# A due-time planner that keeps transfers in order: its backward pass, two TensorE costs and one buffer's clock changed

## The chip, the cores and the metric

The kernel runs on 1 core of one Trainium2 chip. The time is the device time of one execution in microseconds (us). Engines: PE is TensorE, DVE VectorE, ACT ScalarE, POOL GpSimd; SP is SyncE, whose queue issues nearly all DMA transfers.

## The reference

One decoder step on 512 prompt tokens and 8 sample tokens (one new token of each of 8 sequences with 2048 past tokens), all in float32:

```python
h = rmsnorm(x); z = h @ w_in                      # 1024 -> 2840 columns
q, ck, cv, sk, sv, wk, wv, gate, dq, dk, dv = split(z)
o_nsa  = gate0 * compressed + gate1 * selected + gate2 * window   # 8 heads, blocks chosen by top-k
o_diff = rmsnorm((softmax(Q1 K1) - lam * softmax(Q2 K2)) V)       # 4 heads
x = x + concat(o_nsa, o_diff) @ w_out
u = rmsnorm(x) @ w_up; c = causal_conv3(u); a, b = split(c)
x = x + (silu(a) * b) @ w_down
y = rmsnorm(x)                                    # and the new K/V rows and conv states
```

The sample tokens attend to paged caches (16 pages of 128 tokens per sequence, found through a page table): K and V pages of the differential heads, pages of the compressed and selected branches, and a window buffer.

## The kernel before, in words

Activations lie transposed, 520 token columns in two halves of 260. Each float32 operand is split into a high and a low part (xh, xl; wh, wl), and each product is three matmuls: xh wh, xl wh, xh wl. A tile of weights (128 columns of w_in, 512 KB) is loaded into one of three raw buffers (wr, ring RAWR), ACT copies its high part (wh), and DVE or POOL subtracts that for the low part (wl) into a ring of pairs (WH). The in-projection has 22 such tiles and one of the gate (w_g).

Beside the in-projection, PE takes the scores of the sample queries on the K pages (Qzd on kp; 128 pages of 256 KB, two to a kp tile, 7 kp tiles in ring KS), and behind it those on the cp pages (Qzs on cp) and the compression of the cp pages: products of split pages (wh, wl) with w1h and w1l, 256 columns each, and narrow rows of the prompt's own compression (phk with w1h and w1l, 132 and 66 columns). Then come attention, V pages (vp), and the out-projection. From there on (`wout`, `up`, `down`, from L2305) the code is in a fixed order.

All that is ahead of it is written as generators ("processes", `p_...`), each of which yields steps: an engine, a model duration, and the events it sets. `p_wraw` (L909) loads weights, `p_wprep` (L922) splits them, `p_inproj` (L977) multiplies, `p_kload` (L1003) loads K pages, `p_k` (L1017) scores four of them a step, `p_load` (L1217) loads cp pages, `p_stage2` (L1182) small weights, `p_vload` V pages, `p_win` the window buffer. Class `Issue` (L257) runs them on a model of the engines: `run` (L355) takes, among the steps of the engine that is free first, the one with the least `urgency` (L347), that is, its due time from the plan, for PE with a price for a turn from one kind of matmul to another. `used` (L691) tells the model from when on a buffer that the hand-written start has used is free.

`latest` (L403) makes the due times: it goes backward through the steps done, and gives each the latest start with which the model's end stays the same:

```python
        late, free, plan = [end] * len(self.done), dict.fromkeys(self.free, end), {}
        for n in range(len(self.done) - 1, -1, -1):
            name, k, eng, t0, t1, after = self.done[n]
            t = late[n] - (t1 - t0)
            free[eng] = plan[name, k] = t
            for m, lag in after:
                late[m] = min(late[m], t - lag)
```

Only dependences count there: `free` is written and not read, so two transfers on one queue may get the same due time. `kernel` (at the end of the file) builds the program 8 times with the plan of the time before, then 60 times with the best plan and random changes of its due times (0.3 us), and issues the one with the least model end.

Of the kernel before, what the change touches and what calls it, by code (L numbers as in the profile page):

```python
# [41 lines left out]
T_G = 22  # L42
# [214 lines left out]
class Issue:  # L257
# [15 lines left out]
            "qp": 0.14}  # L273
    STICK = 30.0

    IDLE = 0.15

    def __init__(self, plan=None, stuck=False):
# [76 lines left out]
    def run(self):  # L355
        while self.procs:
            ready = []
            for p in list(self.procs):
                if p["op"] is None:
                    if not self.ready(p):  # L360
                        continue
                    self.step(p)
                    if p["op"] is None:
                        continue
                ops = p["op"][0]
                o = min(ops, key=lambda o: self.start(p, o) + o[1]) if isinstance(ops, list) else ops
                ready.append((self.start(p, o), p, o))
            if not ready:
                if self.stuck:
                    raise Planned(float("inf"), None)  # L370
                raise RuntimeError("the processes wait for one another" + str([
                    (p["name"], p["gen"].gi_frame.f_code.co_name, p["gen"].gi_frame.f_lineno,
                     p["gen"].gi_yieldfrom and p["gen"].gi_yieldfrom.gi_frame.f_code.co_name,
                     p["gen"].gi_yieldfrom and p["gen"].gi_yieldfrom.gi_frame.f_lineno)
                    for p in self.procs if p["op"] is None]))
            first = min(ready, key=lambda x: x[0])
            t, p, o = min((x for x in ready if x[2][0] == first[2][0] and x[0] <= first[0] + self.IDLE),
                          key=lambda x: (self.urgency(x[1], x[2], x[0]), x[0], x[1]["name"]))
            sets = p["op"][1:]
            o[2]()  # L380
            end = t + o[1]
            if o[0] == "pe":
                end += self.turn(p)
                self.last = self.KIND.get(p["gen"].__name__, "r")
            self.free[o[0]] = end
            if self.shares(o):
                self.port = end

            if p["of"] is not None:
                p["after"].append((p["of"], (self.AFTER[p["eng"]] if p["eng"] != o[0] else 0.0) + p["pause"]))  # L390
            n = len(self.done)
            self.done.append((p["name"], p["k"], o[0], t, end, p["after"]))
            p["after"], p["pause"], p["of"], p["k"] = [], 0.0, n, p["k"] + 1
            p["t"], p["eng"], p["op"] = end, o[0], None
            for s in sets:
                if isinstance(s, Slot):
                    s.got.t = -50.0
                else:
                    s.t, s.eng, s.of = end, o[0], n
            self.now = end  # L400
            self.step(p)

    def latest(self):  # L403

        end = max(d[4] for d in self.done)
        late, free, plan = [end] * len(self.done), dict.fromkeys(self.free, end), {}
        for n in range(len(self.done) - 1, -1, -1):
            name, k, eng, t0, t1, after = self.done[n]
            t = late[n] - (t1 - t0)
            free[eng] = plan[name, k] = t  # L410
            for m, lag in after:
                late[m] = min(late[m], t - lag)
        return plan
# [7 lines left out]
def _build(tc, T, plan, last):  # L421
# [3 lines left out]
    def mm(out, l, r, start, stop):  # L425
        te.matmul(out, l, r, start=start, stop=stop)  # L426
# [59 lines left out]
    def ps(role):  # L486
        b = ROLE[role][turn[role] % len(ROLE[role])]
        turn[role] += 1
        return PSP(f"bank{b}", [128, 512])
# [137 lines left out]
    t0, t1, t2 = ORDER[:3]  # L627
# [55 lines left out]
    WH, HX, QU, RAWR, ZR, TM, SQ = Ring(2), Ring(2), Ring(4), Ring(3), Ring(3), Ring(2), Ring(2)  # L683
# [4 lines left out]
    def E(*key):  # L688
        return ev.setdefault(key, Event())

    def used(ring, n, t=None):  # L691

        slots = [ring.slot() for _ in range(n)]
        for sl in slots:
            sl.got.t, sl.done.t = -50.0, t
        return slots
# [244 lines left out]
    def new_z(t):  # L941

        if t in T_Q:
            return qu[T_Q.index(t)], None
        if t in T_DV or t in (T_SV, T_WV):
            return zst[t], None
        return None, ZR.slot()

    def blocks(acc, t, hf, ks):
        wh, wl = prep[t]  # L950
        c = slice(hf * HC, (hf + 1) * HC)
        if t == T_G:

            for k in ks:
                w = slice(k * 64, k * 64 + 56)
                mm(acc[:56, :HC], wh[:, w], xh[:, k, c], k == 0, False)
                mm(acc[:56, :HC], wh[:, w], xl[:, k, c], False, k == KT - 1)
            return
        for k in ks:
            w = slice(k * 128, k * 128 + 128)  # L960
            mm(acc[:, :HC], wh[:, w], xh[:, k, c], k == 0, False)
            mm(acc[:, :HC], wh[:, w], xl[:, k, c], False, False)
            mm(acc[:, :HC], wl[:, w], xh[:, k, c], False, k == KT - 1)

    def p_evac(t, z, zsl, accs, slots):
        m = 56 if t == T_G else 128
        if zsl:
            yield zsl
            zsl.got.t = -50.0
            z = X("z", [128, NT], F32, 3)  # L970
        for hf in (1, 0):
            c = slice(hf * HC, (hf + 1) * HC)
            yield E("accs", t, hf)
            yield ("dve", tdve(HC), lambda: tt(ve, z[:m, c], accs[hf][:m, :HC], rstd[:m, c], OP.mult), PS), slots[hf].done
        yield from p_after(t, z, zsl)

    def p_inproj():  # L977
        for n in range(3, NIN):
            t = ORDER[n]
            z, zsl = new_z(t)  # L980
            accs, slots = {}, {}
            if n > 3:
                yield E("w", n)
            for hf in (1, 0):
                sl = slots[hf] = ACC.slot()
                yield sl
                for k in range(KT):
                    def f():
                        if k == 0:
                            accs[hf] = ps("acc")  # L990
                        blocks(accs[hf], t, hf, [k])
                    sets = (sl,) if k == 0 else ()
                    if k == KT - 1:
                        sets = (E("accs", t, hf),) + ((whslot[n].done,) if hf == 0 else ())
                    yield (("pe", 0.24 if t == T_G else 0.36, f),) + sets
                if hf:
                    Q.spawn(p_evac(t, z, zsl, accs, slots), 1, Q.now, "pe")


    kslots, kslot = {}, {}  # L1000
# [14 lines left out]
    NKP = 2  # L1015

    def p_k():  # L1017
        for h in range(4):
            yield E("Qzd", h)
        for i in range(0, NSLOT, NKP):  # L1020
            qd, b = i // 16, (i // 2) % 8
            if i % 16 == 0:
                sl = KB.slot()
                yield sl
                box = {}
            for n in range(i, i + NKP):
                yield E("kp", n)

            def f():
                if i % 16 == 0:  # L1030
                    box["p"] = ps("k")
                for n in range(i, i + NKP):
                    hf = n % 2
                    for h in range(4):
                        mm(box["p"][32 * h:32 * h + 32, 256 * hf:256 * hf + 256], Qzd[:, h, 32 * b:32 * b + 32],
                           kslots[n][:, :, h * 128:(h + 1) * 128], b == 0 and hf == 0, b == 7 and hf == 1)
            yield ((("pe", 0.45 * NKP + 0.1, f),) + tuple(kslot[n].done for n in range(i, i + NKP))
                   + ((sl,) if i % 16 == 0 else ()))
            if (i + NKP) % 16 == 0:
                Q.spawn(p_kout(qd, box["p"], sl), 2, Q.now, "pe")  # L1040

        def f():
            KR.close()
            RAW[0] = Pool(tc, "R0", side="right")
        yield (None, 0.0, f), E("R0")

    def p_kout(qd, kd, sl):
        yield ("act", tact(512), lambda: act(Sd[:, 512 * qd:512 * qd + 512], kd)),
        yield ("dve", tdve(512), lambda: ve.tensor_reduce(out=fac[:, qd:qd + 1], in_=kd, axis=AX.X, op=OP.max), PS), \
            sl.done, E("kd", qd)  # L1050
# [72 lines left out]
    blocks(acc0[t2, 1], t2, 1, range(KT))  # L1123
    used(RAWR, 3, -10.0)
    used(RAWR, 1, -2.2)
    used(WH, 3, -5.0)
    whslot[3] = used(WH, 1)[0]
    used(KS, 4, -10.0)
    used(ZR, 4, -10.0)
# [1446 lines left out]
```

## Time and profile before

| | |
|---|---|
| median of 3 runs | 923.12 us (922.76 to 923.97) |
| profiled execution | 923.06 us |
| its span | 921.2 us |
| its mean granted clock of PE | 0.990 |
| PE busy | 899.1 us |
| DVE, ACT, POOL busy | 573.5, 384.4, 168.3 us |
| bytes moved | 179.83 MB, mean 195 GB/s |

The span runs from the first to the last instruction; the execution has 1.9 us around it. A row of a timeline has its start, its length, engine, line, operation, output and inputs, the number of instructions it stands for, and in brackets how long the engine stood idle before it and what ended that. Matmuls overlap: a row's length is longer than the distance to the next one.

### The profile page before, as it was taken

How to read it: one execution, taken by the hardware profiler on the slowest of the kernel's cores; microseconds unless marked ns; L12 is line 12 of the kernel's file. 1: busy time of each engine (PE TensorE's matmuls, PEld its weight loads, DVE VectorE, ACT ScalarE, POOL GpSimd, SP SyncE). 2: the span in 40 equal slices, each digit the busy share in tenths (PEclk: the TensorE clock that was granted, in tenths of full speed). 3: DMA queues.
4: the chain of work that ended last, by engine and by line, in shares of the span. 5: the costliest groups of instructions: out<-in, count | busy, mean ns of one | idle time of the engine just before them, and what ended most of it. 6: DMA issues, size and time to landing. Idle time of an engine off the chain costs nothing.

```text
span 921.2 us, 22310 instructions
## 1 busy us (share of the span) xinstructions
PE 899.1 (98%) x8628; PEld 805.7 (87%) x8628; DVE 573.5 (62%) x1362; ACT 384.4 (42%) x790; POOL 168.3 (18%) x342
## 2 busy tenths in 40 slices
PE   8999999999999999999998999999999999999996
PEld 5998888889999856656578999999999999999995
DVE  7697563365768696768854667777777777311233
ACT  5256331254555564565652234444444444211120
POOL 5221110000111100101113442111112121224230
PEclk9999999989999999999999999999999999999998
DMA  7749999997777599898733522222222222433322
GB/s 265 241 145 369 347 361 354 320 297 240 227 244 229 207 372 376 291 338 286 246 123 134 150 95 102 92 93 92 93 92 93 92 93 63 151 105 119 104 76 94
DMA packets 86060, 179.83 MB, mean 195 GB/s; under 512 B 10049, under 2 KB 28994, under 8 KB 85954
## 3 DMA queue, kind: packets, MB, share of 16 engines
q1 hardware_dynamic: 85954, 178.41, 56.4%
q8 instruction: 68, 1.11, 0.5%
q14 instruction: 38, 0.31, 0.1%
HBM read 165.78 MB, written 12.59 MB: 194 GB/s over the span
## 4 chain that ended last, share of the span: by engine, by line
PE 89%; DMA 4%; DVE 3%; issue 2%; SPq 1%; ACT 1%; POOL 0%; POOLq 0%; DVEq 0%
PE bank L426 85%; PE bank L1896 3%; DMA kp<-in_kpg 2%; SPq L527 1%; DMA kcT<-vn 1%; DVE bank L1835 1%; DMA cp<-in_cpg 1%; DMA wr<-in_w_in 0%; PE bank L557 0%; DMA vp<-in_vpg 0%; DVE y L438 0%; PE bank L1707 0%; DVE wl L435 0%; ACT gh L429 0%; ACT xh L429 0%
## 5 line engine op out<-in xcount | busy, mean ns | idle before, releaser
L426 PE MATMUL bank<-gl,wh 128*128 128x260 f32 x704 | 199.0, 283 | 0.0
L426 PE MATMUL bank<-gh,wl 128*128 128x260 f32 x704 | 198.9, 283 | 0.0
L426 PE MATMUL bank<-gh,wh 128*128 128x260 f32 x704 | 198.9, 282 | 0.0
L429 ACT ACTIVATE wh<-wr 128x1024 fp32r<-128x1024 f32 (+2 forms) x94 | 96.9, 1030 | 190.2 <-PE bank L426 162.8
L435 DVE TENSOR_TENSOR wl<-wr,wh 128x1024 fp32r<-128x1024 f32 (+1 forms) x86 | 111.2, 1293 | 95.9 <-ACT wh L429 95.5
L426 PEld LDWEIGHTS bank<-gh,wh 128*128 128x128 f32 x704 | 132.6, 188 | 0.0
L426 PEld LDWEIGHTS bank<-gl,wh 128*128 128x128 f32 x704 | 132.5, 188 | 0.0
L426 PEld LDWEIGHTS bank<-gh,wl 128*128 128x128 f32 x704 | 132.4, 188 | 0.0
L426 PE MATMUL bank<-xh,wh 128*128 128x260 f32 (+1 forms) x368 | 105.5, 289 | 1.1 <-ACT wh L429 1.1
L426 PE MATMUL bank<-xl,wh 128*128 128x260 f32 (+1 forms) x368 | 104.5, 286 | 1.8 <-DVE xl L438 1.7
L426 PE MATMUL bank<-xh,wl 128*128 128x260 f32 x352 | 100.1, 284 | 0.0
L426 PE MATMUL bank<-hh,wh 128*128 128x260 f32 (+2 forms) x340 | 96.3, 283 | 0.0
L426 PE MATMUL bank<-hh,wl 128*128 128x260 f32 (+2 forms) x340 | 96.1, 283 | 0.0
L426 PE MATMUL bank<-hl,wh 128*128 128x260 f32 (+2 forms) x340 | 96.0, 282 | 0.0
L426 PEld LDWEIGHTS bank<-xh,wh 128*128 128x128 f32 (+1 forms) x368 | 68.9, 187 | 6.8 <-issue 4.5
L438 DVE SCALAR_TENSOR_TENSOR c<-u,cvw,c 128x536 f32<-128x536 f32 x88 | 69.6, 791 | 2.8 <-ACT c L429 1.3
L426 PEld LDWEIGHTS bank<-xl,wh 128*128 128x128 f32 (+1 forms) x368 | 68.9, 187 | 2.6 <-DVE xl L438 2.5
L426 PEld LDWEIGHTS bank<-xh,wl 128*128 128x128 f32 x352 | 66.9, 190 | 0.0
L426 PEld LDWEIGHTS bank<-hh,wl 128*128 128x128 f32 x340 | 64.1, 188 | 0.0
L426 PEld LDWEIGHTS bank<-hh,wh 128*128 128x128 f32 x340 | 64.0, 188 | 0.0
L441 DVE TENSOR_TENSOR u<-bank,rst 128x260 f32<-128x260 f32 x132 | 40.0, 333 | 38.6 <-PE bank L426 33.0
L426 PEld LDWEIGHTS bank<-hl,wh 128*128 128x128 f32 x340 | 64.0, 188 | 0.0
(392 smaller groups left out, 1913.3 us busy)
## 6 DMA issues: line engine op xcount, KB each, us to landing
vp<-in_vpg SPq DMA_DIRECT2D x128, 320.0 KB, 5.5
kp<-in_kpg SPq DMA_DIRECT2D x128, 256.0 KB, 5.4
cp<-in_cpg SPq DMA_DIRECT2D x128, 192.0 KB, 3.9
wr<-in_w_up SPq DMA_DIRECT2D x44, 512.0 KB, 3.2
wr<-in_w_in SPq DMA_DIRECT2D x21, 512.0 KB, 5.5
wr<-in_w_down SPq DMA_DIRECT2D x16, 512.0 KB, 3.4
out_zT<-z SPq DMA_DIRECT2D x14, 260.0 KB, 5.5
wr<-in_w_down SPq DMA_DIRECT2D x8, 384.0 KB, 3.1
```

Source lines behind the costliest of these rows:

```text
L426: te.matmul(out, l, r, start=start, stop=stop)
L429: se.activation(out=out, in_=in_, func=func, **kw)
L435: eng.tensor_tensor(out=out, in0=a, in1=b, op=OP.subtract)
L438: ve.scalar_tensor_tensor(out=out, in0=a, scalar=s, in1=b, op0=o0, op1=o1, **kw)
L441: eng.tensor_tensor(out=out, in0=a, in1=b, op=op)
L527: sy.dma_start(out=dst, in_=src[bass.ds(numbers[k][i - k], 1)].rearrange("o p f -> (o p) f"))
L1835: ve.tensor_tensor_reduce(out=x, in0=x, in1=cm[:, S - n:], scale=-SC, scalar=3e38, op0=OP.add, op1=OP.min, accum_out=W[i][:, g, q:q + 1])
L1896: te.transpose(p[:, j * 128:(j + 1) * 128], PB[i, g, q][0][:, k * 128:(k + 1) * 128], ident)
```

## The change

In `latest`, a step now carries the name of its generator instead of its engine. For the steps of six generators that move data, the due time is also held under that of the chained step behind it, less its own duration. The model's cost of an in-projection step goes from 0.36 to 0.357 us, that of a step of four K pages from 1.0 to 0.89 us (NKP is 2). Of the three pairs of weight buffers that the start has used, one now comes free at 0.7 in the model's time instead of -5.0.

```diff
+    CHAINED = ("p_kload", "p_wraw", "p_load", "p_stage2", "p_vload", "p_win")
...
-            self.done.append((p["name"], p["k"], o[0], t, end, p["after"]))
+            self.done.append((p["name"], p["k"], p["gen"].__name__, t, end, p["after"]))
...
-        late, free, plan = [end] * len(self.done), dict.fromkeys(self.free, end), {}
+        late, queue, plan = [end] * len(self.done), end, {}
         for n in range(len(self.done) - 1, -1, -1):
-            name, k, eng, t0, t1, after = self.done[n]
+            name, k, of, t0, t1, after = self.done[n]
             t = late[n] - (t1 - t0)
-            free[eng] = plan[name, k] = t
+            if of in self.CHAINED:
+                t = queue = min(t, queue - (t1 - t0))
+            plan[name, k] = t
...
-                    yield (("pe", 0.24 if t == T_G else 0.36, f),) + sets
+                    yield (("pe", 0.24 if t == T_G else 0.357, f),) + sets
...
-            yield ((("pe", 0.45 * NKP + 0.1, f),) + tuple(kslot[n].done for n in range(i, i + NKP))
+            yield ((("pe", 0.44 * NKP + 0.01, f),) + tuple(kslot[n].done for n in range(i, i + NKP))
...
-    used(WH, 3, -5.0)
+    used(WH, 2, -5.0)
+    used(WH, 1, 0.7)
```

The program's instructions are the same otherwise; the new due times put them in another order. Lines behind L403 lie 5 or 6 further down in the change.

DVE at the start, the kernel before: the split of the fourth tile of weights (wl_407) ahead of the second tile's evacuation (z_402) and of the first tile's rope (dq0_77, and sq_482 for the sample columns):

```order
L441 TENSOR_TENSOR z_401<-bank0_221,rstd_127 128x260
L435 TENSOR_TENSOR wl_407<-wr_404,wh_406 128x1024
L441 TENSOR_TENSOR z_402<-bank3_224,rstd_127 128x260
L441 TENSOR_TENSOR z_402<-bank2_223,rstd_127 128x260
L774 COPY sq_482<-z_401 32x8 x4
...
L717 COPY dq0_77<-z_401 32x520 x4
L441 TENSOR_TENSOR dq0_77<-dq0_77,sin_129 128x520
```

DVE at the start, the change:

```order
L446 TENSOR_TENSOR z_401<-bank0_221,rstd_127 128x260
L779 COPY sq_457<-z_401 32x8 x4
...
L722 COPY dq0_77<-z_401 32x520 x3
L446 TENSOR_TENSOR z_402<-bank3_224,rstd_127 128x260
L446 TENSOR_TENSOR z_402<-bank2_223,rstd_127 128x260
L446 TENSOR_TENSOR z_403<-bank6_226,rstd_127 128x260
L446 TENSOR_TENSOR dq0_77<-dq0_77,sin_129 128x520
L440 TENSOR_TENSOR wl_407<-wr_404,wh_406 128x1024
L446 TENSOR_TENSOR dq0_77<-dq0_77,tmp_488 128x520
```

The split has moved behind nearly all of the first tile's rope.

SP where the gate's weights (w_g) are loaded, the kernel before (an ISA row sets a page's address):

```order
L527 DMA kp<-in_kpg 128x512
L511 DMA wr<-in_w_g 128x512
L511 DMA wr<-in_w_in 128x1024 x3
L527 ISA
L527 DMA kp<-in_kpg 128x512
```

The change:

```order
L532 DMA kp<-in_kpg 128x512
L516 DMA wr<-in_w_in 128x1024
L516 DMA wr<-in_w_g 128x512
L532 ISA
L532 DMA kp<-in_kpg 128x512
```

Three tiles of weights stood behind w_g and ahead of the next pages; now one stands ahead of w_g, and eight pages follow.

PE right behind the in-projection, the kernel before (z_91 with Qcn ends the scores on new rows):

```order
L426 MATMUL bank_2590<-z_91,Qcn 32x8 x2
L426 MATMUL bank_2606<-cp,Qzs 32x128 x4
L426 MATMUL bank_2619<-phk,w1h_115 128x132
L426 MATMUL bank_2619<-phk,w1l_116 128x66
...
L426 MATMUL bank_2606<-cp,Qzs 32x128 x4
```

The change:

```order
L431 MATMUL bank_2609<-z_91,Qcn 32x8 x2
L431 MATMUL bank_2623<-cp,Qzs 32x128 x4
L431 MATMUL bank_2637<-wh,w1h_115 128x256
L431 MATMUL bank_2637<-wl,w1h_115 128x256
L431 MATMUL bank_2637<-wh,w1l_116 128x256
...
L431 MATMUL bank_2702<-phk,w1h_115 128x132
L431 MATMUL bank_2702<-phk,w1l_116 128x66
L431 MATMUL bank_2637<-wh,w1h_115 128x256
```

The products of 256 columns have moved ahead, with the phk rows scattered among them.

## Rows read from the trace of the kernel before

**Rows 1.** The profile's page: busy us of the engines, and the chain that ended last, by engine.

```profile
PE 899.1 (98%) x8628; PEld 805.7 (87%) x8628; DVE 573.5 (62%) x1362; ACT 384.4 (42%) x790; POOL 168.3 (18%) x342
...
PE 89%; DMA 4%; DVE 3%; issue 2%; SPq 1%; ACT 1%; POOL 0%; POOLq 0%; DVEq 0%
```

**Rows 2.** Windows of the whole span, 50 us each and the rest: from and to, length, busy us (and instructions) of PE, weight loads, DVE, ACT, POOL, then PE's granted clock, the DMA engines' busy share, and GB/s.

```profile
50.00:100.00 50.00, 49.23 (x505) 43.06 (x505) 36.25 (x83) 29.63 (x56) 7.33 (x7) 1.00 0.82 289
...
150.00:200.00 50.00, 48.44 (x462) 41.14 (x461) 20.57 (x55) 17.54 (x38) 1.89 (x11) 0.93 0.96 334
...
300.00:350.00 50.00, 47.28 (x670) 35.53 (x668) 39.65 (x156) 27.67 (x89) 5.25 (x11) 1.00 0.82 301
...
500.00:921.20 421.20, 411.34 (x3421) 410.10 (x3419) 239.15 (x406) 141.51 (x171) 101.08 (x212) 0.99 0.30 99
```

**Rows 3.** PE's waits, by what ended them: us in total, times, the longest.

```profile
PE bank L426 <- DMA cp<-in_cpg: 1.3, 2, 1.0
...
PE bank L426 <- ACT p L429: 1.1, 1, 1.1
PE bank L426 <- DMA kp<-in_kpg: 1.0, 2, 0.8
...
PE bank L426 <- DMA vp<-in_vpg: 0.8, 3, 0.4
```

**Rows 4.** DVE's timeline from 20 to 45 us.

```profile
32.86 1.23 DVE L435 TENSOR_TENSOR wl<-wr,wh 128x1024 fp32r<-128x1024 f32 x1 [2.73 <-ACT wh L429]
...
43.21 0.69 DVE L441 TENSOR_TENSOR dq<-dq,tmp 128x520 f32<-128x520 f32 x1
...
43.90 0.76 DVE L441 TENSOR_TENSOR z<-bank,rstd 128x260 f32<-128x260 f32 x2
```

**Rows 5.** PE's timeline from 43 to 45 us.

```profile
44.46 0.36 PE L426 MATMUL bank<-xh,wh 128*128 128x260 f32 x1 [1.11 <-ACT wh L429]
```

**Rows 6.** PE's timeline at three bursts of K-page scores.

```profile
60.47 0.28 PE L426 MATMUL bank<-xl,wh 128*128 128x260 f32 x1
60.59 0.28 PE L426 MATMUL bank<-xh,wl 128*128 128x260 f32 x1
60.80 2.80 PE L426 MATMUL bank<-kp,Qzd 128*32 128x256 f32 x48
...
63.75 0.28 PE L426 MATMUL bank<-xl,wh 128*128 128x260 f32 x1
...
85.94 0.64 PE L426 MATMUL bank<-kp,Qzd 128*32 128x256 f32 x8 [0.77 <-DMA kp<-in_kpg]
...
172.72 0.28 PE L426 MATMUL bank<-xh,wl 128*128 128x260 f32 x1
172.93 1.93 PE L426 MATMUL bank<-kp,Qzd 128*32 128x256 f32 x32
...
175.02 0.28 PE L426 MATMUL bank<-xl,wh 128*128 128x260 f32 x1
```

**Rows 7.** Windows beside the K pages, columns as in rows 2.

```profile
45.00:60.00 15.00, 15.00 (x128) 15.00 (x127) 13.53 (x43) 9.61 (x20) 4.22 (x7) 1.00 0.30 105
...
120.00:140.00 20.00, 20.00 (x198) 17.86 (x191) 12.97 (x20) 4.76 (x7) 2.99 (x2) 1.00 1.01 365
140.00:160.00 20.00, 19.74 (x212) 16.64 (x211) 6.46 (x9) 3.69 (x4) 0.00 (x0) 1.00 0.98 349
```

**Rows 8.** The timeline of SP's DMA issues, at the gate's weights and at the first cp pages (a row's length runs from its first issue to its last).

```profile
42.31 0.34 SPq L511 DMA_DIRECT2D wr<-in_w_g  x1
49.09 8.70 SPq L511 DMA_DIRECT2D wr<-in_w_in  x3
...
173.15 7.07 SPq L527 DMA_DIRECT2D cp<-in_cpg  x12
```

**Rows 9.** PE's timeline from 181 to 194 us.

```profile
182.08 0.42 PE L426 MATMUL bank<-cp,Qzs 128*32 128x128 f32 x8
182.44 0.33 PE L426 MATMUL bank<-phk,w1h 128*128 128x132 f32 x1
...
184.12 0.41 PE L426 MATMUL bank<-cp,Qzs 128*32 128x128 f32 x2 [0.25 <-DMA cp<-in_cpg]
...
187.48 2.17 PE L426 MATMUL bank<-cp,Qzs 128*32 128x128 f32 x8 [1.05 <-DMA cp<-in_cpg]
189.58 0.48 PE L426 MATMUL bank<-phk,w1h 128*128 128x132 f32 x1
...
190.03 0.56 PE L426 MATMUL bank<-wh,w1h 128*128 128x256 f32 x1
...
193.73 0.28 PE L426 MATMUL bank<-wl,w1h 128*128 128x256 f32 x1
```

**Rows 10.** Windows from 186.8 us on, columns as in rows 2.

```profile
186.84:193.67 6.83, 6.20 (x26) 4.71 (x27) 5.11 (x12) 5.45 (x12) 0.00 (x0) 0.50 1.05 387
193.67:200.50 6.83, 6.83 (x64) 6.59 (x63) 4.22 (x16) 3.28 (x10) 0.76 (x6) 1.00 0.80 251
```

**Rows 11.** DVE's timeline at the out-projection: additions of the residual.

```profile
494.45 0.43 DVE L441 TENSOR_TENSOR z<-bank,z 128x260 f32<-128x260 f32 x1 [9.78 <-PE bank L426]
...
496.49 0.75 DVE L441 TENSOR_TENSOR z<-bank,z 128x260 f32<-128x260 f32 x2
```

**Rows 12.** PE's timeline at the same place.

```profile
495.02 0.36 PE L426 MATMUL bank<-dq,wh 128*128 128x260 f32 x1 [0.26 <-DVE z L441]
```

## The prediction

> **What bounds the kernel now.** I read the page's head first [rows 1]: TensorE (PE) is busy 899.1 of 921.2 us, and the chain that ended last is 89% PE. So a reordering can only win back the 22 us in which PE stands, or a stretch in which PE runs slowly. The windows of 50 us come next [rows 2]. The stretch behind 500 us, written out by hand and the same in both kernels, holds 421.2 - 411.3 = 9.9 us of the idle time. That leaves some 12 us ahead of it, part of it the start-up, which is also the same in both. [...] The window from 300 shows 2.7 us idle. Third, the list of PE's waits [rows 3] says what it stood for: cp pages 1.3 us, K pages 1.0, a probability tile p 1.1, V pages 0.8. None is large. Then I took PE's timeline at each of these places, and VectorE's (DVE's) and the DMA queue's (SP's) beside it; those rows are quoted with the terms below.
>
> The change adds no instruction to the chip's work. It gives other due times to the planner, which puts the same matmuls, splits and transfers in another order. So each term is a wait or a turn that the new order brings or takes, and the sum is made against the profiled execution, 923.06 us (span 921.2 and 1.9 around it); the median of the runs, 923.12, is the same within 0.06.
>
> **Early splits (a).** Before, DVE stands 2.73 us for the split of the fourth tile of weights, and works off the evacuations and the rope behind it afterwards: the rope of the first tile ends with the row at 43.21, only then is a z buffer free, and the evacuation at 43.90 follows [rows 4]. PE waits 1.11 us for its bank at 44.46 [rows 5]; the row names ACT, but ACT's split serves a later matmul. In the new order the rope of the first tile stands ahead of that split, so DVE uses the 2.73 us and is earlier at 43. At best all of the 1.11 goes. At worst a new wait of the same size comes, because the split itself is now behind the rope. I take -0.7, nearer to the gain, since the idle time is longer than the rope pieces moved into it; ends -1.1 and +1.1.
>
> **Round trips to the K pages (b).** The K-score matmuls are put between those of the in-projection in bursts. A burst of 24 instructions (48 in the trace, two passes each) takes 60.59 to 63.75 = 3.16 us between in-projection matmuls that otherwise start 0.12 apart; less two such steps, 2.92. A burst of 16 takes 172.72 to 175.02 = 2.30, less 0.24 is 2.06 [rows 6]. So 8 instructions (4 pages) cost 0.86, and each round trip costs 2.92 - 3 x 0.86 = 0.34. The order has 11 bursts before, ten of 24 and one of 16, and 18 in the change, nine of them of only 8. That is 7 x 0.34 = **+2.4**; ends 2.0 and 2.6 for the rounding of the rows.
>
> **Waits for K pages (c).** The first burst stands behind 111 fewer in-projection matmuls, so it comes at 60.80 - 111 x 0.12 - 0.7 = 46.8. From there to the second half of the 13th burst PE has 314 in-projection matmuls (37.7), 16 units (13.8) and 12 round trips (4.1): 55.6 us. In the same time 58 pages of 256 KB, seven tiles of weights and the gate's weights have to come, 19.1 MB. The DMA moved 365 and 349 GB/s in the two full windows, and only 105 between 45 and 60, where the old order has few pages to fetch [rows 7]: there the queue issues w_g at 42.31 and then waits for a raw buffer until 49.09, so no page passes it [rows 8]. At 357 GB/s the 19.1 MB take 53.5 us, 2 us less than PE has. That cover is about one page's way from issue to landing, so I can't tell a gain from a loss and take 0. Ends: -1.0, all K waits gone [rows 3], and +2.4, the difference between 19.1 MB at 365 and at 349. The K waits seen so far did not cost the clock: the 0.77 us at 85.94 [rows 6] lies in a window with a granted clock of 1.00 [rows 2].
>
> [...]
>
> **The stretch behind the in-projection (d, e).** Before, the last K burst leaves only 42 in-projection matmuls, the cp pages are issued from 173.15 on [rows 8], and PE then has only narrow work: groups on 132 and 66 columns, scores on cp, and two waits for cp of 0.25 and 1.05 us [rows 9]. The order shows why: between the score groups stand phk rows alone. The granted clock is 0.50 from 186.8 to 193.7 and 1.00 behind it [rows 10]. A score group (8 in the trace) takes 182.08 to 182.44 = 0.36 at the full clock and 187.48 to 189.58 = 2.10 at half: 1.74 lost. The 16 products from 190.03 to 193.73 take 3.70, where 16 x 0.12 = 1.92 would do: 1.78 lost. Together 3.5. In the change 147 in-projection matmuls, 105 more or 12.6 us, stand behind the last K burst, so the cp pages have that much more time, and the 256-column products start right behind the first score group, with phk rows only here and there. I take **-1.3** for the waits (d; the other end 0) and **-3.5** for the clock (e; the other end 0).
>
> [...]
>
> **Attention (f).** The window from 300 holds 2.7 us idle [rows 2], of which p and the V pages are 1.1 and 0.8 [rows 3]. In the change the first score units of the attention stand ahead of the first V pages instead of behind 41 rows of them, which gives the exponentials more room. Much else there is shuffled as well. I take -0.5; ends -2.7 (all idle time goes) and +1.9 (the two waits come a second time).
>
> **Out-projection (g).** DVE adds the first half tile early, the second at 494.45, when PE's last bank is done [rows 11], and PE goes on at 495.02 behind a wait of 0.26 us [rows 12]. In the new order the first bank too gets its last matmuls at the end, so both additions are in the chain: two take 0.75, one 0.43 [rows 11], **+0.3**.
>
> Sum: -0.7 + 2.4 + 0 - 1.3 - 3.5 - 0.5 + 0.3 = -3.3, and 923.06 - 3.3 = **919.8 us**. The costs edited in the planner (0.357, 0.89, the third buffer at 0.7) cost nothing on the chip; they act through this order alone.
>
> **The rivals.** R1, no change: PE's lower clock moves instead of going. Behind the products the new order has another cluster without wide matmuls (68 rows: scores on cp, hy, qu and vn rows). If the clock falls there, 3.5 come back: 919.8 + 3.5 = 923.3. For it: the old fall came in just such work. Against it: that cluster has its transfers behind it and no cp wait of 1.05 us.
>
> R2, slower: the short K bursts are paced by their pages. The queue carries pages and weights at 349 rather than 357 GB/s, PE runs dry in bursts of 8, 2.4 us of waits come, and PE once falls to half rate for as long as before, 3.5: 919.8 + 5.9 = 925.7. It decides if the landings fall behind by more than the 2 us of cover in (c). For it: PE's need (55.6) and the supply (53.5) are nearly even. Against it: the queue starts on the pages sooner, and in-projection matmuls lie between the bursts.
>
> R3, faster still: K waits (1.0) and all the attention's idle time (2.2 more) go too: 919.8 - 3.2 = 916.6. For it: the transfers are ordered to leave room for those behind. Against it: V's waits lie where pages come at PE's pace.
>
> That the change does nothing is out: the three places of the order differ.
>
> **How the numbers follow.** A measurement of this kernel can tell about 0.2% from no change, 1.85 us: faster is below 921.27, slower above 924.97. The forecast has 0.50, R1 0.22, R2 0.16, R3 0.12. The forecast's own range, from (a), (c), (f), is about 917.5 to 922. Faster: 0.41 of the forecast, 0.03 of R1, all of R3, 0.56. Same: 0.08 + 0.16 + 0.04 of R2 = 0.28. Slower: 0.01 + 0.03 + 0.12 = 0.16. The range reaches from R3's value to between R1 and R2: 916.5 to 925.0, which leaves out about half of R3 and most of R2's upper part.
>
> **What would show it.** (a) No PE wait over 0.5 us between 30 and 47. (b) 18 K bursts, and PE at the last of them some 12 us further ahead of the in-projection's end. (c) K waits in PE's list between 0 and 2.4. (d, e) No cp wait and a granted clock of 1.00 between 170 and 200; a half-clock stretch anywhere ahead of 500 speaks for R1 or R2, by whether K bursts or narrow matmuls stand ahead of it. (f) Under 2.7 us idle around the first attention units. The forecast is wrong if the first out-projection row behind the wait at 495.02 [rows 12] isn't some 3 us earlier, since from there on both kernels run the same code.

## The result and the profile after

The change is slower: 932.52 us (median of 4, 930.23 to 934.55) against 922.98 (median of 4), a ratio of 1.0103 with a 95% interval of 1.0084 to 1.0121. The forecast was 919.8 us, with 925.0 as the range's upper end.

The profiled execution is the slowest of the four, 934.55 us with a span of 932.7, 11.5 more than before. Its page: PE's busy time rose by 5.8 us, so it was not waits alone.

```profile
PE 904.9 (97%) x8628; PEld 806.8 (86%) x8628; DVE 581.1 (62%) x1371; ACT 377.9 (41%) x784; POOL 168.0 (18%) x339
```

Windows of 50 us (columns as in [rows 2]): the clock that was 0.93 between 150 and 200 is 1.00 there now, but 0.97 between 200 and 250, and 400 to 450 has 3.5 us idle, where before had 1.0 (the row by itself).

```profile
50.00:100.00 50.00, 48.97 (x515) 39.54 (x508) 38.98 (x76) 20.70 (x43) 7.73 (x7) 1.00 0.97 354
...
150.00:200.00 50.00, 50.00 (x491) 46.96 (x489) 23.21 (x56) 17.31 (x36) 3.57 (x14) 1.00 0.91 303
200.00:250.00 50.00, 48.05 (x457) 44.76 (x456) 28.06 (x88) 24.12 (x72) 4.13 (x24) 0.97 0.69 222
...
400.00:450.00 50.00, 46.50 (x617) 27.12 (x605) 31.83 (x104) 26.66 (x76) 2.93 (x3) 1.00 0.91 317
```

```profile
400.00:450.00 50.00, 48.96 (x606) 28.93 (x604) 39.07 (x130) 30.38 (x89) 3.02 (x3) 1.00 0.88 300
```

PE's waits, against [rows 3]: cp has left the list's head and p its place; kp and vp are more than twice as long. The longest is kcT<-vn (the newest row of a sequence's window values, written into its buffer by a transfer), 2.5 us where before had 0.3 (the second list); a wait of 1.2 us for qu is new.

```profile
PE bank L431 <- DMA kcT<-vn: 2.5, 2, 1.5
PE bank L431 <- DMA kp<-in_kpg: 2.3, 3, 1.0
PE bank L431 <- DMA vp<-in_vpg: 2.2, 4, 0.8
```

```profile
PE bank L426 <- DMA kcT<-vn: 0.3, 1, 0.3
```

To find where the 11.5 us lie I cut both traces at the same work: the end of the setup (its statistics matmul), the last in-projection matmul, and the first matmul of the FFN. The part behind that is 394 us in both. Two windows, before (the first stretch is the in-projection with the K pages, the second all else up to the FFN):

```profile
28.04:180.78 152.74, 150.60 (x1497) 133.63 (x1496) 95.43 (x192) 57.10 (x93) 21.47 (x23) 1.00 0.87 307
180.78:526.97 346.19, 338.29 (x3787) 268.85 (x3786) 239.87 (x762) 180.27 (x517) 45.53 (x104) 0.99 0.74 251
```

and the change:

```profile
29.69:186.20 156.51, 153.19 (x1498) 134.24 (x1496) 103.22 (x207) 50.78 (x85) 24.98 (x24) 1.00 0.88 310
186.20:538.81 352.61, 340.05 (x3788) 268.12 (x3787) 239.73 (x755) 179.91 (x519) 42.42 (x100) 1.00 0.71 241
```

The setup took 1.65 us more (29.69 against 28.04), the first stretch 3.8, the second 6.4. The setup's part is not the change's: a kernel with the change's order (the last but one below) has 28.30; from 16 to 20 us the granted clock is 1.00 there and 0.50 in the change. So two losses are to be explained, and the second, in which I had forecast a gain of 5 us, is the larger.

### The profile page after: what moved, and what is told of

It reads as the page before. It is cut to its first block, busy times and chain, and to the rows that moved or that the text cites. A ratio compares the mean times of both kernels' runs of the same rounds, so it can differ in the third digit from the quotient of the medians.

```text
span 932.7 us, 22310 instructions
## 1 busy us (share of the span) xinstructions
PE 904.9 (97%) x8628; PEld 806.8 (86%) x8628; DVE 581.1 (62%) x1371; ACT 377.9 (41%) x784; POOL 168.0 (18%) x339
## 3 DMA queue, kind: packets, MB, share of 16 engines
q8 instruction: 68, 1.11, 0.5%
## 4 chain that ended last, share of the span: by engine, by line
PE 83%; DMA 6%; DVE 5%; issue 2%; SPq 2%; ACT 1%; POOL 0%; POOLq 0%; DVEq 0%
PE bank L431 80%; PE bank L1902 2%; DMA kp<-in_kpg 1%; DMA kcT<-in_winv 1%; DMA kcT<-vn 1%; DMA vp<-in_vpg 1%; SPq L532 1%; DMA wr<-in_w_in 1%; DVE sq L779 1%; DVE z L446 1%; DMA cp<-in_cpg 0%; DVE dq L722 0%; DVE sq L446 0%; DVE wl L440 0%; SPq L630 0%
## 5 line engine op out<-in xcount | busy, mean ns | idle before, releaser
L440 DVE TENSOR_TENSOR wl<-wr,wh 128x1024 fp32r<-128x1024 f32 (+2 forms) x85 | 108.8, 1280 | 96.1 <-ACT wh L434 95.1
```

What stands on the lines that cost most here:

```text
L440: eng.tensor_tensor(out=out, in0=a, in1=b, op=OP.subtract)
```

## The experiments

The theories. A: the chain costs the time in the attention, by V pages and window buffers. B: the cheaper TensorE costs do it. C: any new search of the plan lands anywhere, everywhere (a draw, below, is the order that one search finds). D, formed after the first four runs: the chain on K pages and weights lengthens the first stretch; the second is the luck of the drawn order. E: the planner's lag from a transfer's issue to its data (2.0 us) is too short. F: the second loss follows from the first. G: the window rows wait in the one queue behind V pages.

All kernels in one table: the two stretches and the K bursts (counted on PE's timeline) are those of the profiled execution, the ratio is to the kernel before on the same chip. Executions of one kernel on one chip lie 1.2 to 7.8 us apart, and a stretch is read from one of them: chain alone's is the fastest of five (924.6 us, median 926.9), the change's the slowest of four. So a few us between two stretches are less sure than the ratios.

| kernel | chained | K bursts | first stretch | second stretch | median us | ratio (95%) |
|---|---|---|---|---|---|---|
| before | none | 11 | 152.7 | 346.2 | 923.0 | |
| change | all six | 18 | 156.5 | 352.6 | 932.5 | 1.0103 (1.0084 to 1.0121) |
| costs alone | none | 11 | 151.1 | 346.0 | 921.8 | 0.9990 (0.9979 to 1.0001) |
| chain alone | all six | 14 | 157.1 | 342.0 | 926.9 | 1.0051 (1.0027 to 1.0074) |
| before, seed 1 | none | 11 | 151.5 | 353.3 | 929.2 | 1.0070 (1.0053 to 1.0087) |
| change, seed 1 | all six | 16 | 160.5 | 350.9 | 935.1 | 1.0119 (1.0102 to 1.0136) |
| chain on K, weights | two | 12 | 155.4 | 352.8 | 933.0 | 1.0109 (1.0081 to 1.0137) |
| chain on others | four | 11 | 148.9 | 355.3 | 929.1 | 1.0055 (1.0035 to 1.0075) |
| change, lag 5.0 | all six | 21 | 156.9 | 349.3 | 930.4 | 1.0072 (1.0050 to 1.0095) |
| change's first, costs' rest | | 19 | 157.0 | 346.7 | 927.8 | 1.0061 (1.0034 to 1.0087) |
| costs' first, change's rest | | 11 | 150.3 | 357.2 | 930.8 | 1.0067 (1.0044 to 1.0089) |
| others' first, chain alone's rest | | 11 | 148.8 | 348.6 | 924.0 | 1.0008 (0.9991 to 1.0026) |
| costs alone, seed 1 | none | 11 | 154.3 | 345.8 | 925.4 | 1.0021 (1.0004 to 1.0037) |
| change, window on ACT's queue | all six | 18 | 156.9 | 358.6 | 939.0 | 1.0158 (1.0126 to 1.0190) |
| others' first, costs' rest | | 11 | 148.6 | 351.7 | 924.6 | 1.0009 (0.9993 to 1.0024) |

Below each, its two windows, columns as in [rows 2].

**Costs alone** (edits against the change)

```diff
-    CHAINED = ("p_kload", "p_wraw", "p_load", "p_stage2", "p_vload", "p_win")
+    CHAINED = ()
-    used(WH, 2, -5.0)
-    used(WH, 1, 0.7)
+    used(WH, 3, -5.0)
```

> The two cheaper TensorE costs alone, no chained transfers, the third buffer as before. If the chain in the backward pass costs the time (theory A), this is not slower than before: 919 to 924 us, and the attention waits of the change (kcT<-vn 2.5 us, vp 2.2 us) are not there. If the cheaper costs do it by more and shorter K bursts (theory B), it is 928 us or more with 15 or more K bursts. If any new search of the plan lands anywhere (theory C), it may come out on either side, and the stages where it loses are others than in the change.

```profile
28.16:179.29 151.13, 150.01 (x1497) 133.95 (x1496) 96.42 (x194) 57.23 (x94) 22.67 (x23) 1.00 0.86 308
179.29:525.26 345.97, 338.28 (x3787) 269.05 (x3786) 239.64 (x759) 179.94 (x517) 45.58 (x104) 0.99 0.74 252
```

As A says, not B: 11 bursts, no loss. Its matmuls behind the in-projection stand in before's order but for three, and the second stretch is the same within 0.2 us, with the same granted clock: here one order took the same time twice.

**Chain alone** (the costs and the buffer as before)

> The chained due times alone, TensorE's costs and the third buffer as before. Theory A: slower by 6 us or more (929 to 934), with waits on kcT<-vn and vp of over 3 us together. Theory B: 921 to 925, with 11 to 13 K bursts. Theory C: anywhere between 918 and 934.

```profile
29.48:186.58 157.10, 152.93 (x1498) 134.92 (x1496) 100.41 (x197) 56.98 (x94) 21.72 (x23) 0.99 0.87 308
186.58:528.53 341.95, 332.74 (x3787) 268.31 (x3786) 239.93 (x759) 179.43 (x518) 45.77 (x99) 1.00 0.73 249
```

Slower, but not where A has it: the second stretch is 4 us shorter than before's, the first 4 longer, with 14 bursts. A (929 or more) and B (925 at most) missed; C's range holds it.

**Before with another seed**, `default_rng(1)` in `kernel`

> The kernel before, with another seed for the random changes of its due times; nothing else. Theories A and B: within 3 us of before (920 to 926). Theory C, luck of the search: more than 3 us away, on either side.

```profile
28.13:179.63 151.50, 150.30 (x1497) 133.72 (x1496) 94.31 (x193) 58.38 (x95) 20.23 (x22) 1.00 0.87 309
179.63:532.92 353.29, 340.76 (x3787) 270.02 (x3786) 237.58 (x752) 180.22 (x521) 48.62 (x107) 0.99 0.72 246
```

This one says most. Nothing of the change is in it, and the second stretch is 7 us longer than before's, as much as in the change. A and B missed.

**The change with another seed**, the same edit

> The whole change with another seed. Theories A and B: again slower, 927 to 937 us, and in the same stage (waits in the attention). Theory C: it may be anywhere from 917 to 934, with waits at other places than with the first seed.

```profile
28.06:188.57 160.51, 154.50 (x1497) 135.66 (x1496) 98.83 (x200) 56.10 (x93) 23.45 (x23) 0.99 0.86 304
188.57:539.51 350.94, 339.37 (x3787) 267.44 (x3786) 239.01 (x749) 179.78 (x520) 49.22 (x106) 1.00 0.71 242
```

Slower again: A's and B's 927 to 937 us came, C's upper end of 934 was passed by 1 us. The first stretch is again over 155 us. So theory D: the two stretches have two causes.

**Chain on K pages and weights only, and on the other four only**

```diff
-    CHAINED = ("p_kload", "p_wraw", "p_load", "p_stage2", "p_vload", "p_win")
+    CHAINED = ("p_kload", "p_wraw")                             # and, in the other kernel:
+    CHAINED = ("p_load", "p_stage2", "p_vload", "p_win")
```

> The change, but only the K-page loads and the raw weight loads are chained; the other four kinds of transfer are not. Theory D (the chain on these two makes the in-projection stage longer, by short K bursts and waits; what is behind it is the luck of the plan): the stretch from the setup's end to the in-projection's end is 155 to 160 us (before 152.7, costs alone 151.1) with 14 or more K bursts. Theory A (the chain on V pages and window buffers costs the time in the attention): that stretch may be long, but the stretch from there to the first matmul of the FFN is 344 to 348 us as before (346.2), not 352.6 as in the change.

```profile
28.62:184.06 155.44, 152.01 (x1497) 135.13 (x1496) 99.81 (x198) 54.49 (x89) 21.67 (x23) 0.99 0.88 307
184.06:536.83 352.77, 341.24 (x3787) 270.56 (x3786) 236.40 (x750) 180.83 (x522) 49.22 (x108) 0.99 0.72 244
```

> The change, but the K-page loads and the raw weight loads are not chained; the other four kinds are. Theory D: the first stretch is 150.5 to 152.5 us with 11 or 12 K bursts, and the stretch behind it anything from 341 to 353; in all 916 to 927 us. Theory A: the stretch behind is 350 us or more, with waits on kcT<-vn and vp of 4 us or more; 925 us or more.

```profile
28.23:177.12 148.89, 148.62 (x1491) 132.96 (x1490) 95.53 (x195) 55.32 (x91) 22.13 (x22) 1.00 0.91 318
177.12:532.46 355.34, 341.72 (x3794) 271.91 (x3792) 239.00 (x760) 178.47 (x518) 46.84 (x104) 0.98 0.72 244
```

The long first stretch goes with the chain on K pages and weights (155.4), and is gone without it (148.9, with only 0.3 us idle; six rows for the gate, 0.8 us, stand behind the cut there). In the first kernel the bursts were 12, not the 14 or more that I expected; its loss is in waits (3.4 us idle) and in the lower clock from 40 to 45 us (0.66) rather than in turns. In the second kernel A's forecast came true in full: 355.3 us behind, waits on kcT<-vn and vp of 1.7 and 3.5 us, 929.1 in all; D missed with all three numbers (148.9, 355.3, 929.1). What speaks against A is that first kernel, 352.8 us where A gave 344 to 348, and before with another seed: both are long without a chain on V pages and window buffers. So the chain isn't needed for a long second stretch; that it adds nothing to one is not shown.

**The change with a lag of 5.0 us**

```diff
-    AFTER = {"pe": 0.22, "act": 0.06, "dve": 0.08, "pool": 0.1, "dma": 2.0, None: 0.0}
+    AFTER = {"pe": 0.22, "act": 0.06, "dve": 0.08, "pool": 0.1, "dma": 5.0, None: 0.0}
```

> The whole change with one more edit: the planner believes that a transfer's data is there 5.0 us after its issue instead of 2.0 (the profile's median for K and V pages is 5.4 and 5.5). Theory E (the chain lets transfers come just in time by a lag that is too short): PE's waits on kp, vp, cp and kcT<-vn fall from 7.7 us in all to under 3, and the time is 922 to 928 us. Theory D: those waits may fall, but the first stretch stays 155 us or longer for its K bursts, and the time is 926 us or more.

```profile
28.45:185.35 156.90, 155.06 (x1497) 135.51 (x1496) 96.19 (x195) 58.84 (x98) 22.38 (x23) 0.99 0.90 313
185.35:534.64 349.29, 338.94 (x3788) 269.13 (x3787) 236.29 (x754) 181.42 (x523) 38.77 (x97) 0.98 0.71 242
```

Its waits:

```profile
PE bank L431 <- DVE nsc L446: 3.4, 2, 1.9
PE bank L431 <- DVE wl L440: 3.2, 2, 1.8
```

Half right. PE waits for no transfer any more (7.7 us in the change: kcT, kp, vp and cp), as E says, though the longer lag also made a new draw. Waits for DVE took their place, and the time stayed over E's 922 to 928, in D's 926 or more.

**Two orders put together.** A kernel runs two searches, and replays the order of the in-projection's processes (roots 0 to 8) from one and of the rest from the other:

```diff
+    (p1, e1), (p2, e2) = search(*FIRST), search(*REST)
+    Issue.STICK = 0.0
+    plan = {x: p1[x] if x[0][0] < 9 else p2[x] + e1 - e2 for x in p1}
+    nc = once(plan, True)
```

> A kernel that runs both searches, takes the order of the in-projection stage (its weights, splits, matmuls, K pages) from the change and the order of all other work from the kernel with the cheaper costs alone. Theory D, the two parts add: the first stretch is 155 to 157.5 us as in the change (156.5), the stretch behind 345 to 349 as with costs alone (346.0), 925 to 930 us in all. Theory F, the loss behind the in-projection comes of how the early transfers leave the queue: the stretch behind is over 351 here.

```profile
28.22:185.24 157.02, 153.19 (x1497) 134.21 (x1496) 104.32 (x209) 50.27 (x84) 23.75 (x23) 1.00 0.89 311
185.24:531.90 346.66, 338.20 (x3788) 266.84 (x3786) 238.21 (x755) 178.08 (x513) 47.19 (x107) 1.00 0.72 245
```

> The other way round: the in-projection's order from the kernel with the cheaper costs alone, the rest from the change. Theory D: the first stretch is 150.5 to 152 us, the stretch behind 351 to 355 (352.6 in the change), 926 to 931 us in all. Theory F: the stretch behind is 344 to 348, and the time 919 to 924.

```profile
28.21:178.52 150.31, 149.89 (x1497) 133.91 (x1496) 94.74 (x194) 56.97 (x93) 21.88 (x22) 1.00 0.88 310
178.52:535.72 357.20, 343.74 (x3787) 267.70 (x3786) 241.69 (x758) 182.99 (x526) 39.94 (x97) 1.00 0.72 244
```

D's main test, and it holds in kind: the change's first stretch with the other's rest is 157.0 and 346.7, the reverse 150.3 and 357.2. F as stated is out: an early part without the chain doesn't mend the second stretch. But 357.2 is over D's 351 to 355. PE waits 1.3 us for cp pages there, and score groups of 8 on cp take up to 1.58 us (below) in place of some 0.43, at a granted clock of 1.00: the first cp page is issued 7.2 us ahead of the in-projection's end, where in the change it is 18.6, so the change's rest meets late pages. (Some 5% of the rows behind the place where the two orders meet also stand elsewhere than in their own kernel.)

```profile
184.65 1.58 PE L432 MATMUL bank<-cp,Qzs 128*32 128x128 f32 x8
```

> The in-projection's order from the kernel that chains the other four transfers (148.9 us), the rest from the kernel with the chain alone (341.9 us). Theory D: 148.5 to 150 and 341 to 346 us, 914 to 919 us in all, faster than before. Theory F: the stretch behind goes back to 350 or more, and the time is 922 or more.

```profile
29.04:177.88 148.84, 148.65 (x1492) 132.98 (x1490) 94.94 (x194) 55.34 (x91) 21.91 (x22) 1.00 0.92 320
177.88:526.52 348.64, 338.63 (x3794) 271.03 (x3792) 239.72 (x760) 180.66 (x521) 48.34 (x102) 0.99 0.73 247
```

The first stretch came over whole, but of the second's good draw (342.0) only part did: 348.6 and 924.0 are both outside D's ranges. No better than before.

> The cheaper costs alone, no chain, another seed. Theory D: the first stretch stays at 150 to 152.5 us with 11 or 12 K bursts; the stretch behind is a new draw, anywhere from 341 to 355, so 916 to 930 us. Theory A: the stretch behind is 344 to 348.

```profile
28.04:182.31 154.27, 150.38 (x1498) 133.75 (x1496) 93.77 (x193) 58.26 (x95) 22.80 (x23) 1.00 0.86 301
182.31:528.09 345.78, 337.55 (x3787) 267.28 (x3786) 234.97 (x746) 181.33 (x525) 51.16 (x108) 1.00 0.74 253
```

The second stretch (345.8) fits D and A. The first is a miss that corrects D: without the chain it too can draw waits (3.9 us idle here). PE's busy time in it, 150.4, stays at that of the other kernels with 11 bursts.

**Window transfers on ACT's queue**, in the change's order

```diff
-            yield ("dma", 0.75, lambda: sy.dma_start(out=win(b), in_=T["winv"][b])),
+            yield ("dma", 0.75, lambda: se.dma_start(out=win(b), in_=T["winv"][b])),
...
-            yield ("dma", 0.05, lambda: sy.dma_start(out=win(b)[127:128, 3], in_=vn[b:b + 1, 0])), E("win", b)
+            yield ("dma", 0.05, lambda: se.dma_start(out=win(b)[127:128, 3], in_=vn[b:b + 1, 0])), E("win", b)
```

(and the third, out_swv, alike)

> The change in its own order on every engine, but the 24 transfers of the window buffer (kcT<-in_winv, kcT<-vn, out_swv<-kcT) are issued on ACT's queue, not on SP's behind the V pages. If the 2.5 us that PE waits for kcT<-vn come of the one queue (theory G), these waits fall under 0.5 us, the stretch behind the in-projection is 348 to 351 us instead of 352.6, and the time is 928 to 931 us. If they come of the order alone (the rows are due too late, theory D), the waits stay over 1.5 us and the time within 2 us of the change's 932.5.

```profile
28.30:185.24 156.94, 153.28 (x1498) 134.29 (x1496) 103.32 (x207) 50.79 (x85) 25.05 (x24) 1.00 0.90 312
185.24:543.85 358.61, 341.47 (x3787) 267.53 (x3786) 240.99 (x755) 180.63 (x519) 42.57 (x100) 1.00 0.71 237
```

Its longest wait of PE:

```profile
PE bank L431 <- DMA kcT<-vn: 5.1, 6, 1.6
```

G falls: the waits doubled to 5.1 us. D's second half missed too: the order is the change's, and the time is 6.5 us over it. What these waits consist of is shown under (f); why they are longer on ACT's queue stays open.

**Others' first, costs' rest**

> The in-projection's order from the kernel that chains the other four transfers (148.9 us), the rest from the kernel with the cheaper costs alone (346.0 us). Theory D, the parts add up to the perturbation seen where two orders meet (0.7 and 4.6 us behind): 148.5 to 150 and 346 to 350 us, 918 to 923 us in all, faster than or like before. Theory F: the stretch behind is over 351, and the time over 925.

```profile
28.25:176.81 148.56, 148.56 (x1492) 132.98 (x1490) 95.41 (x195) 55.34 (x91) 21.92 (x22) 1.00 0.91 319
176.81:528.51 351.70, 340.72 (x3794) 270.73 (x3792) 239.84 (x761) 179.60 (x515) 46.20 (x106) 0.99 0.73 246
```

The first stretch is the best there is, with no idle time; what it gains (4 us) the second loses again, 5.5 us over before, with 4.3 us of waits in the compression, behind the place where the two orders meet (1.9 with costs alone). Of D's ranges only the first stretch came; F's second stretch (over 351) came, its time (over 925) not quite. So the parts don't simply add: in all three kernels with a shorter first stretch than their rest had come with, the second grew, by 4.6, 6.7 and 5.7 us, and by 0.7 in the one with a longer first stretch. Part of what a short first stretch gains is paid back behind it; how much in general isn't shown. No kernel here beats the one before beyond its interval.

## Why the prediction was wrong, by its steps

**(a) Early splits: inside its ends.** The wait of 1.11 [rows 5] is gone, and a wait of 0.97 for the sample queries (Qzd) in the first K burst has come, since that burst now runs at 47.8 instead of 60.8: -0.1, where -0.7 was taken. **(c) K waits** rose by 1.3 us, inside -1.0 to +2.4, where 0 was taken. The reason given for the 0 was wrong: the 2 us of cover are less than half of a K page's way from issue to landing, whose median in the trace of before is 5.4 us. PE's timeline of the change:

```profile
49.38 0.40 PE L431 MATMUL bank<-kp,Qzd 128*32 128x256 f32 x1 [0.97 <-DVE Qzd L794]
...
55.23 0.28 PE L431 MATMUL bank<-xh,wl 128*128 128x260 f32 x1
55.44 1.07 PE L431 MATMUL bank<-kp,Qzd 128*32 128x256 f32 x16
...
56.67 0.28 PE L431 MATMUL bank<-xl,wh 128*128 128x260 f32 x1
...
63.11 0.64 PE L431 MATMUL bank<-kp,Qzd 128*32 128x256 f32 x8 [1.03 <-DMA kp<-in_kpg]
...
186.94 0.38 PE L431 MATMUL bank<-wh,w1h 128*128 128x256 f32 x1
...
229.50 0.71 PE L431 MATMUL bank<-hy,w2p 128*128 128x128 f32 x4 [1.19 <-DVE qu L1684]
...
231.99 0.42 PE L431 MATMUL bank<-wl,w1h 128*128 128x256 f32 x1
232.21 0.42 PE L431 MATMUL bank<-wh,w1l 128*128 128x256 f32 x1
...
415.96 0.30 PE L431 MATMUL bank<-kcT,Sw 128*32 128x128 f32 x1 [1.47 <-DMA kcT<-vn]
```

**(b) Round trips: right in mechanism and size.** A burst of 8 takes 55.23 to 56.67 = 1.44, less two steps of 0.12, 1.20 = 0.86 + 0.34, as worked out. PE's busy time in the first stretch rose by 2.6 (forecast 2.4), and it goes with the bursts: 149.9 to 150.6 in the five kernels with 11 of them and the in-projection's full 1497 or 1498 rows, 153.2 and 153.3 with 18 or 19. (The four with 12, 14, 16 and 21 bursts have 152.0, 152.9, 154.5 and 155.1, each with 3.4 us at half clock in it; less half of that, an estimate, 150.3, 151.2, 152.8 and 153.4.) (a), (b) and (c) together explain the first loss: -0.1 + 2.6 + 1.3 = 3.8. That it goes with the chain on K pages and weights, the draws show: 155.4 to 160.5 us in the five with it, 148.9 to 154.3 in the five without. That the chain works by spacing the pages' due times one load apart, so that single steps of four pages come due between in-projection steps, I only read from the code, and the kernel with 12 bursts has its loss without many turns.

**(d) was right, (e) half of it, as R1 had it.** The products stand at 186.94, right behind the first scores, no cp wait of 1 us is left, and the half-clock stretch at 187 is gone (granted clock 1.00 from 186.41 to 226.98). But at 231.99 matmuls of 256 columns start 0.21 apart at a granted clock of 0.51, half rate again, for about half as long as before, behind a wait of 1.19 us in a cluster of narrow work. The window there, and below it the same work in the kernel with window transfers on ACT's queue, where PE has the same order and the same wait of 1.19 us (at 228.39):

```profile
231.63:235.00 3.37, 3.37 (x19) 3.37 (x18) 2.73 (x10) 0.83 (x2) 0.00 (x0) 0.51 0.00 0
```

```profile
230.00:235.00 5.00, 5.00 (x43) 5.00 (x44) 4.64 (x15) 2.33 (x7) 0.82 (x3) 1.00 0.01 4
```

Of the 3.5 us some 1.7 came back (half of 3.37), so (e) gave -1.8. But the second window has the full clock: the fall in that cluster is not fixed by the order, so R1's fall came in this kernel's execution and not in that one's. K bursts did not bring it: with K waits up to 1.03 us, the clock between 50 and 100 us stayed 1.00. That narrow work makes the clock fall and that wide products hold it up, on which I took -3.5 for (e), no run shows: this cluster had 0.51 in the one execution and 1.00 in the other.

**(f) Attention: the step that failed.** I wrote "Much else there is shuffled as well. I take -0.5", with +1.9 as the upper end. By difference it was +7.5: the second stretch's +6.4, less (d) -0.9, (e) -1.8 and (g) +0.4, and less 1.2 for the other waits in the compression (qu 1.2 and hx 0.4 are new, one of 0.3 is gone). Waits make about 4 of it (kcT<-vn 2.5 where before had 0.3, vp 2.2 where it had 0.8, and small ones on DVE and ACT). The rest, 3.5 us, is PE's busy time, and its cause stays open: in the second stretch PE goes from one pair of operands to another 1559 times before and 1573 times in the change, but 1596 times in chain alone, which has the least busy time of all (332.7). Where the largest wait comes from, the chain that ended last shows in the change's trace (start, length, and what ran):

```profile
404.48 5.10 DMA kcT<-in_winv
...
409.64 6.27 DMA kcT<-vn
...
424.23 7.32 DMA kcT<-in_winv
431.57 5.08 DMA kcT<-vn
```

Two transfers stand one behind the other: the window's values land at 409.58, the new row, which overwrites part of them, is issued only then, at 409.64, and PE goes on at 415.96, 11.5 us after the first issue. In `p_win` the planner counts 0.75 + 5.0 + 0.05 up to the row's issue and 2.0 from there to its data, 7.8 us. With a lag of 5.0 in place of 2.0 PE doesn't wait for it.

The deeper error stands behind the number. I priced the places that I could see in the trace of before and took the rest of a reshuffled order as neutral. It was not: in the nine drawn orders that ran (before and costs alone count as one), the second stretch is 342.0, 345.8, 346.0, 349.3, 350.9, 352.6, 352.8, 353.3 and 355.3 us. Before's is the third best, the middle is 350.9, so by these nine a new draw was worth some +5 us (an estimate) ahead of any argument on its parts. Part of the spread is the clock, which one order did not fix (0.51 and 1.00 in the cluster above): others chained and lag 5.0 have 13.7 us at half clock in that stretch, before 6.8, the change 3.4, chain alone none. Chained or not makes no difference that these nine can show: 342.0 to 355.3 with V pages and windows chained, 345.8 to 353.3 without. **(g)** was right: the waits for z at the out-projection rose from 1.4 to 1.8, +0.4 for +0.3. The sign named for the whole forecast was clear: the first out-projection row behind the wait at 495.02 [rows 12] stands at 506.80 in the change, 11.8 us later and not 3 earlier.

R2 had the sign and a price of 925.7, but the wrong place: K bursts did wait (+1.3), the clock did not fall there.

## What to carry to other kernels

When a change makes a search draw a new order, the first question is how far draws of the old code lie apart: a run with another seed here moved the time by 6 us, two thirds of the change's effect, and no view of the old trace shows it. Cut the traces at the same work and compare stretches, since one cause can sit in the first and luck in the second. A good order that an old search came upon is not kept by new rules: of the eight other draws here one has a shorter second stretch than before (342.0), one the same (345.8), and six have longer ones.

## What the runs showed that I had not expected

A stretch at half clock was not tied to an order here. The change and the kernel with window transfers on ACT's queue have the same order on PE but for a few rows, and from the cut to 226 us they take the same within 0.13 us; then the one has 3.4 us at half clock at 231.7, the other at 440.6. In the setup the one has a granted clock of 0.50 from 15 to 20 us and the other 1.00, and it takes 29.69 against 28.30 us, so single executions differ by over 1 us before any of the changed work. Nor does a stretch's length follow from it: costs alone has 6.8 us at half clock in its second stretch, nearly the same rest behind the change's in-projection has none, and they take 346.0 and 346.7.
